# A DeepNorm layer with attention and retention heads: the norm of a retention head in two parts, key scaling and gating on ScalarE, gate rows turned by TensorE, first column sums read from the bank

## The chip, the core and the metric

The kernel runs on one core of a Trainium2 chip. A core has five engines that run side by side, each through its own list of instructions in order: TensorE (PE) multiplies matrices, VectorE (DVE), ScalarE (ACT) and GpSimd (POOL) work on tiles of 128 partitions, and SyncE (SP) issues transfers to 16 DMA engines. Results of PE land in PSUM, in banks of 128 x 512 float32, and a bank can be written again only when its readers are done. The metric is the device time of one execution in microseconds (us).

## The reference

One decoder layer over 1024 positions of width 1024, in float32. The part that the change touches is the conditioning and the retention heads:

```
mod = silu(c) @ w_ada + b_ada              # six rows of 1024: sh1, sc1, g1, sh2, sc2, g2
h = x * (1 + sc1) + sh1
proj = h @ w_in                            # 8 attention heads of 64 and 4 retention heads of 128
# retention, in chunks of 128 positions, per head:
q = q*cos + rotate_half(q)*sin;  k = (k*cos + rotate_half(k)*sin) * dk**-0.5
s = (q @ k.T) * inner                      # inner: decay of the head
o = s @ v + (q @ R) * xi
R = R * g_chunk + (k * zeta).T @ v
# then, per head and position:
o = (o - mean(o)) * rsqrt(var(o) + eps) * silu(g)
mix = concat(attention, o) @ w_out
x = layer_norm(alpha*x + g1*mix)           # then a gated MLP with a convolution, gated by g2, and a second norm
```

## The kernel before

A float32 product is made of three matmuls: each operand is split into a high and a low part in a format that PE multiplies at full rate, and high x high, high x low and low x high are added up in a bank. The low part of a weight or of h is a subtraction on DVE or POOL after a cast on ACT.

The program has one block (named r) that computes the conditioning, the four retention heads and the value projection of the attention heads; attention itself, the output projection and the MLP follow. Only block r is touched. Two things set the order in it. PE's instructions, most of DVE's and some of ACT's and SP's are chained in the order in which the code issues them (by `queued`, which shows as line 150 in the profile; `in_turn`, `turn` and `vec` call it). The others, among them ACT's copies out of the banks and POOL's products, are placed by a scheduler.

The block goes through these stages.

- **The condition row.** silu(c) stands in eight columns. DVE multiplies the identity by each column (tile `diag`), a matmul with ones spreads that as a row over all partitions (`csp`, a double bank), and ACT copies the two halves to `csb`. Before and after it PE multiplies a constant tile (`warm`) 6 and 11 times (`keep_on`).
- **The first head's first seven chunks** (`h_load`, `h_cast`, `h_sum`, `h_mod`, `h_lo`, `h_low`). For each j of 8 (128 features each), SP loads two pieces of w_ada (tiles `ada`, 512 KB each), 128 rows of the first head's weights (`wrr`) and of x transposed (`xt`). DVE sums ada times csb over the row into a column of scales and one of shifts (`h_sum`; it shows as ISA or CUSTOM_DVE). ACT scales xt into the high part `hhi`, DVE makes `hlo`, and PE adds 21 matmuls (7 chunks x 3) into seven banks (`fa`, `fb`). Near the end SP loads the second head's weights and small tables (`ret_consts`).
- **The retention loop**, m = 7 to 31, a chunk of a head in each. A chunk's projection is 24 matmuls (`rp`) in two half-steps, after each of which `emit(t)` issues what a table holds for half-step t. ACT copies the bank to a row tile `rst` (q, k, v, g, 128 columns each); POOL multiplies q and k by the sine (`rt`, lines 372 and 373), and DVE by the cosine and adds (`ret_spin`). `ret_a` turns q and k on PE (`pq`), copies them on ACT (`qkT`) and scales k by the decay on DVE (`kz`). `ret_b` multiplies k with q and kz with v (`pS`), and DVE makes `sT` (scores times decay) and the state `R`. `ret_c` makes the output `po`, from which DVE takes the mean and variance (`bs`, `mv`) and ACT a copy. `ret_swish` is a tanh on ACT and a product on DVE. At a head's end `ret_norm` makes the scale of its eight chunks (17 operations on 128x8 on DVE: `gt`, `gr`, `wg`), `ret_gate` normalises a chunk on DVE and multiplies it with its gate on POOL (line 464), and `ret_out` turns four chunks (`py`) and stores them. `mod_piece` sums one piece of the other four conditioning rows (`ada`) from step m = 10 on.
- **The value projection**, q = 0 to 15: 24 matmuls in a bank `vp`, from which ACT casts the high part and DVE subtracts the low part for four heads (`V`, lines 621 and 622). In the same steps come the last retention operations, the last column sums, and the load, cast and low part of the first attention head's weights (`wqkr`, `wqh`, `wql`).

The two rows g1 and g2 are needed as rows much later. They come out of the sums as columns (`gcol`, 128 x 8) and are stored by a transfer to `gates` that puts each element at its place.

The table of half-steps is made by these lines:

```
    A0, N0, O0, O1 = 3, 5, 3, 5
        ta = max(2 * n + A0, 2 * NT - 1 + (5 * n + 3) // 4)
        tb = ta + 1
        t_c = tb + (2 if late else 1)
```

where n counts a head's chunks through all heads, ta is the half-step of `ret_a`, tb of `ret_b`, t_c of `ret_c`. Within a half-step the operations are issued in the order of RANK.

## Time and profile before

| | |
|---|---|
| median of 3 runs | 1247.38 us (1246.58 to 1248.6) |
| the profiled execution | 1248.95 us, span 1247.2 us |
| mean granted clock of TensorE | 0.990 |
| PE busy | 1210.4 us, 97% of the span |
| DVE, ACT, POOL busy | 923.7, 631.4, 249.8 us |
| block r | from 0 to about 300 us: PE busy for 281.38 us of them |

The profile is of one execution. A line of a group or of the timeline names the kernel's line, the engine, the operation and the tiles (written tile, arrow, read tiles, without their numbers), then the shape and how many; brackets hold the idle time of the engine before it and what ended that. Lines 150 and 152 are those of the helper `queued`, so that groups there are told apart by tiles. PE is busy nearly all the time, and its clock, PEclk, is granted in parts of full speed: where PE waits, time goes, and after some waits the clock is lower for a while. The other engines' idle time is of no matter by itself.

### The profile page before, as it was taken

The numbers are of one execution on the slowest core, as the hardware profiler recorded it, in microseconds if no ns is written. First come the engines' busy times: TensorE is split into PE (matmuls) and PEld (weight loads), VectorE is DVE, ScalarE is ACT, GpSimd is POOL, SyncE is SP. The second block draws the span as 40 slices with busy tenths as digits, with TensorE's granted clock in tenths as the row PEclk, the third lists the DMA queues.
The fourth block names the chain that finished last, engine by engine and source line by source line (L and its number), as shares of the span: only waits on it lengthen the run. The fifth ranks groups of instructions, "written<-read, shape, count | busy, mean of one in ns | idle before, by whom it ended". The sixth has DMA issues, their size and how long they took to land.

```text
span 1247.2 us, 17036 instructions
## 1 busy us (share of the span) xinstructions
PE 1210.4 (97%) x5982; PEld 1008.4 (81%) x5982; DVE 923.7 (74%) x1784; ACT 631.4 (51%) x1131; POOL 249.8 (20%) x293
## 2 busy tenths in 40 slices
PE   7998999979999999999999999999999999999997
PEld 5887888978888887788788888888888878888885
DVE  7857758574877778746797877878778785886586
ACT  5533232233766668476764544544445554634452
POOL 0315143210333334300002221221100101000021
PEclk9999999989999999999899999999999999999999
DMA  9523344753234235323239877886544578965751
GB/s 355 214 75 120 110 153 136 146 101 111 85 95 151 77 102 180 107 94 109 85 111 227 188 175 202 202 192 179 133 130 132 150 249 247 348 224 192 264 185 68
DMA packets 88261, 199.77 MB, mean 160 GB/s; under 512 B 11952, under 2 KB 18288, under 8 KB 88176
## 3 DMA queue, kind: packets, MB, share of 16 engines
q1 hardware_dynamic: 75504, 175.62, 42.0%
q0 software_dynamic: 12672, 23.07, 11.7%
q8 instruction: 47, 0.77, 0.3%
q14 instruction: 38, 0.31, 0.1%
HBM read 165.06 MB, written 68.20 MB: 187 GB/s over the span
## 4 chain that ended last, share of the span: by engine, by line
PE 80%; DVE 10%; DMA 4%; ACT 3%; issue 2%; POOL 1%; DVEq 0%; SPq 0%; ACTq 0%; POOLq 0%
PE dX L1314 10%; PE rp L150 7%; PE dZ L1314 7%; PE uX L1130 6%; PE uX L1131 6%; PE uX L1132 6%; PE uY L1131 4%; PE uY L1132 4%; PE uY L1130 4%; PE pv L800 3%; PE qk L716 2%; PE qk L717 2%; PE qk L718 2%; PE pt L784 2%; DVE ada L150 2%
## 5 line engine op out<-in xcount | busy, mean ns | idle before, releaser
L150 PE MATMUL rp<-wr,hhi 128*128 128x512 f32 x400 | 129.1, 404 | 0.0
L1303 DVE TENSOR_TENSOR dl<-dr,dh 128x1024 fp32r<-128x1024 f32 x66 | 80.0, 1236 | 36.6 <-ACT dh L1291 36.3
L1291 ACT CAST dh<-dr 128x1024 fp32r<-128x1024 f32 x66 | 67.8, 1049 | 74.1 <-DMA dr<-in_w_down_dram 35.9
L762 POOL TENSOR_TENSOR S<-S,dn 128x128 f32<-128x128 f32 (+3 forms) x64 | 74.1, 1163 | 154.2 <-DVE dn L761 123.8
L977 POOL DMA_DIRECT2D sd<-gd x22 | 18.1, 824 | 397.3 <-DMA sd<-y 231.8
L150 PEld LDWEIGHTS rp<-wr,hhi 128*128 128x128 f32 x400 | 72.3, 190 | 13.0
L150 PE MATMUL rp<-wr,hlo 128*128 128x512 f32 x200 | 79.2, 396 | 0.0
L1314 PE MATMUL dX<-dl,dh 128*128 128x512 f32 x176 | 68.5, 389 | 0.0
L1314 PE MATMUL dX<-dh 128*128 128x512 f32 x176 | 68.5, 389 | 0.0
L1314 PE MATMUL dX<-dh,dl 128*128 128x512 f32 x176 | 68.5, 389 | 0.0
L150 DVE CUSTOM_DVE_ANT_0 ada<-ada,csb,bcol 128x1024 f32<-128x1024 f32 (+1 forms) x48 | 61.7, 1298 | 8.7 <-DMA ada<-in_ada_dram 5.1
L1145 ACT COPY u<-uX 128x512 f32<-128x512 f32 x44 | 25.8, 586 | 74.2 <-PE uX L1132 74.2
L758 ACT ACTIVATE S<-S,mn 128x128 f32<-128x128 f32 (+3 forms) x64 | 49.8, 779 | 15.6 <-DVE mn L753 14.3
L150 PE MATMUL vp<-wv,hhi 128*128 128x264 f32 (+1 forms) x256 | 50.8, 299 | 4.8 <-DVE gt L150 4.8
L716 PE MATMUL qk<-hhi,wqh 128*128 128x512 f32 x128 | 54.6, 427 | 0.0
L753 DVE CUSTOM_DVE_ANT_0 S<-ps,nb 128x128 f32<-128x128 f32 (+3 forms) x64 | 47.9, 750 | 8.4 <-PE ps L751 6.0
L791 DVE TENSOR_TENSOR pt<-pt,pt 128x512 fp32r<-128x512 f32 (+2 forms) x96 | 50.8, 550 | 4.3 <-ACT pt L790 3.1
L800 PE MATMUL pv<-pt,V 128*128 128x256 f32 x320 | 49.9, 293 | 2.4 <-DVE pt L791 1.2
L193 PE MATMUL op<-wol,mxs 128*128 128x512 f32 x128 | 50.4, 394 | 1.7 <-DVE wol L900 1.5
L718 PE MATMUL qk<-hhi,wql 128*128 128x512 f32 x128 | 51.7, 404 | 0.0
L192 PE MATMUL op<-woh,mxs 128*128 128x512 f32 x128 | 50.7, 398 | 0.9 <-DVE mn L753 0.9
L1314 PE MATMUL dZ<-dh 128*128 128x512 f32 x132 | 51.6, 391 | 0.0
(1040 smaller groups left out, 3670.2 us busy)
## 6 DMA issues: line engine op xcount, KB each, us to landing
ada<-in_ada_dram SPq DMA_DIRECT2D x48, 512.0 KB, 4.2
td<-in_w_down_dram SPq DMA_DIRECT2D x44, 256.0 KB, 5.8
wa<-in_w_up_dram SPq DMA_DIRECT2D x22, 512.0 KB, 5.5
wb<-in_w_up_dram SPq DMA_DIRECT2D x22, 512.0 KB, 4.9
gd<-y SPq DMA_DIRECT2D x22, 512.0 KB, 3.2
sd<-y SPq DMA_DIRECT2D x44, 256.0 KB, 3.6
dr<-sd SPq DMA_DIRECT2D x44, 256.0 KB, 3.9
dr<-td SPq DMA_DIRECT2D x44, 256.0 KB, 4.1
```

What stands on the lines that cost most here:

```text
L150: order[key] = fn(*args, **kw)
L716: nc.tensor.matmul(pt, whi[:, j, :], hhi[j][:, sl], start=(j == 0), stop=False)
L718: nc.tensor.matmul(pt, wlo[:, j, :], hhi[j][:, sl], start=False, stop=(j == ND - 1))
L762: nc.gpsimd.tensor_tensor(out=Ssb[:, :span], in0=Ssb[:, :span], in1=den.to_broadcast([P, span]), op=ALU.mult,)
L791: nc.vector.tensor_tensor(out=dl, in0=src, in1=f(dh), op=ALU.subtract)
L800: nc.tensor.matmul(pv[:, :256], V2[h][:, kb, :], pts[kb // 4][u][:, kb % 4, :], start=(kb == 0 and u == 0), stop=(kb == nkb - 1 and u == 1),)
L1130: nc.tensor.matmul(pt, whi, bh, start=start, stop=False, skip_group_check=True)
L1131: nc.tensor.matmul(pt, whi, bl, start=False, stop=False, skip_group_check=True)
L1132: nc.tensor.matmul(pt, wlo, bh, start=False, stop=stop, skip_group_check=True)
L1291: nc.scalar.copy(hi, raw)
L1303: nc.vector.tensor_tensor(out=lo, in0=raw, in1=f(hi), op=ALU.subtract)
L1314: nc.tensor.matmul(pt, w_[:, 0, q], m_[:, 1, :], start=start and n_ == 0, stop=stop and n_ == 2, skip_group_check=True)
```

## The change

The diff touches block r alone, in four places.

1. **Start.** The condition row lies in two tiles, a bank each, and the sums of the first piece read them from PSUM in halves, scale and shift in turn, without waiting for `csb` (`h_sum0`). The constant tile is set by POOL, `keep_on` is 5 and 9 matmuls, the two sums of the next piece go ahead of `h_lo`, and the loads of the second head's weights move forward (`w1_load`): two at j = 4 right behind x's last piece, two among the small tables.
2. **First head.** The sine products of its chunks 0 to 6 (14 operations) go from POOL to DVE, in `ret_spin`.
3. **Retention.** `kz` is made by ACT (28 operations). `ret_norm` is in two parts, one half-step apart: 7 operations, then 10, the last of which is new: mr = -mean x scale. With it a chunk is normalised by one ACT operation, scale x o + mr (32 operations, formerly on DVE). The output product comes two half-steps after the scores for each chunk, sT has three buffers, and in a half-step output, scores and turning come ahead of swish, gates and norm. Gates start two half-steps after the norm's first part, and the two output halves come at 4 and 6.
4. **Gate rows.** The columns of g1 and g2 are turned on PE (after q = 2 and q = 10), copied by ACT, and stored as 8 rows of 512 bytes (`mod_rows`).

DVE's list shows the third place around the first head's norm. In the names, gt, gr and wg are the norm's small tiles, mv the means and variances, mr the new tile, rst the row tiles, ISA with ada a column sum. Before, from the norm's tail to the next scores:

```order
L150 TENSOR_SCALAR wg_1014<-wg_1014 128x8
L150 TENSOR_TENSOR gr_1012<-gr_1012,wg_1014 128x8
L150 TENSOR_SCALAR gr_1012<-gr_1012,rc 128x8
L150 TENSOR_TENSOR rst_2_592<-rst_2_592,trig 128x256
L150 TENSOR_TENSOR rst_2_592<-rst_2_592,rt_5_991 128x2x64 x2
L150 ISA ada_0_3_938,mod_94<-ada_0_3_938,csb,bcol 128x1024
L150 ISA mod_94 128x1
L150 SCALAR_TENSOR_TENSOR rst_0_590<-rst_0_590 128x128
L150 TENSOR_SCALAR rst_0_497<-rst_0_497,mv_501,gr_1012 128x128 x2
L150 TENSOR_TENSOR sT_1_1064<-pS_1_1061,dec 128x128
L150 SCALAR_TENSOR_TENSOR R_1_1066<-R_0_976,rc,pS_1_1061 128x128
```

Here the norm of 17 operations stands in one piece, and a rotation, a column sum, a swish and two gates stand between it and sT. With the change, from a score to the next one:

```order
L152 TENSOR_TENSOR sT_1_1036<-pS_1_1033,dec 128x128
L152 SCALAR_TENSOR_TENSOR R_1_1038<-R_0_964,rc,pS_1_1033 128x128
L152 SCALAR_TENSOR_TENSOR rst_3_499<-rst_3_499 128x128
L152 TENSOR_SCALAR gt_1049<-mv_500,rc 128x8
L152 TENSOR_SCALAR gt_1049<-gt_1049,rc 128x8
L152 TENSOR_SCALAR gr_1050<-gt_1049 128x8
L152 TENSOR_TENSOR wg_1053<-gr_1050 128x8
L152 TENSOR_TENSOR wg_1053<-wg_1053,gt_1049 128x8
L152 TENSOR_SCALAR wg_1053<-wg_1053 128x8
L152 TENSOR_TENSOR gr_1050<-gr_1050,wg_1053 128x8
L152 TENSOR_TENSOR sT_2_1078<-pS_2_1075,dec 128x128
L152 SCALAR_TENSOR_TENSOR R_2_1080<-R_1_1038,rc,pS_2_1075 128x128
```

The norm's first part stands between two sT. Behind these rows come a swish, the second part (ten operations), a rotation and a column sum, then the next sT; no gate is in the list.

ACT's list at the same place of the program has the copies of a turned pair (qkT), the tanh (rst from rst alone), the casts of the third head's weights (wr) and the copies of outputs (rst from po). Before:

```order
L432 COPY rst_0_590<-po_1_1095 128x128
L392 COPY qkT_3_1112<-pq_3_1109 128x256
L439 ACTIVATE rst_1_591<-rst_1_591 128x128
L181 CAST wr_6_1124<-wrr_6_1122 128x512
L181 CAST wr_7_1127<-wrr_6_1122 128x512
L392 COPY qkT_4_1166<-pq_4_1163 128x256
L432 COPY rst_1_591<-po_2_1149 128x128
```

With the change, where L500 is the gate and kz the key scaling:

```order
L430 ACTIVATE kz_4_1148<-rst_2_591,rc 128x128
L426 COPY qkT_3_1085<-pq_3_1082 128x256
L471 ACTIVATE rst_1_590<-rst_1_590 128x128
L500 ACTIVATE rst_0_496<-rst_0_496,mr_1100,gr_1050 128x128 x2
L500 ACTIVATE rst_1_497<-rst_1_497,mr_1100,gr_1050 128x128 x2
L500 ACTIVATE rst_2_498<-rst_2_498,mr_1100,gr_1050 128x128 x2
L500 ACTIVATE rst_3_499<-rst_3_499,mr_1100,gr_1050 128x128 x2
L430 ACTIVATE kz_5_1226<-rst_2_591,rc 128x128
L426 COPY qkT_4_1146<-pq_4_1143 128x256
L471 ACTIVATE rst_2_591<-rst_2_591 128x128
L178 CAST wr_6_1110<-wrr_6_1108 128x512
```

The eight gates of the first head stand together, behind the turned pair of the second head's chunk 3 and ahead of the key scaling of chunk 5, the pair of chunk 4 and the casts of the weights.

SP's list shows the fourth place, in the value projection. Before, the store of the gates stands between column-sum loads and ahead of the load of the first attention head's weights:

```order
L542 DMA ada_3_1_2443<-in_ada_dram 128x1024
L542 DMA ada_3_2_2487<-in_ada_dram 128x1024
L169 DMA gates<-gcol 128x8x1
L542 DMA ada_3_3_2535<-in_ada_dram 128x1024
L542 DMA ada_3_4_2574<-in_ada_dram 128x1024
L591 DMA wqkr_2577<-in_w_qk_dram 128x1024
L542 DMA ada_3_5_2625<-in_ada_dram 128x1024
```

With the change:

```order
L577 DMA ada_3_1_2447<-in_ada_dram 128x1024
L577 DMA ada_3_2_2491<-in_ada_dram 128x1024
L577 DMA ada_3_3_2539<-in_ada_dram 128x1024
L577 DMA ada_3_4_2583<-in_ada_dram 128x1024
L634 DMA wqkr_2586<-in_w_qk_dram 128x1024
L585 DMA gates<-grow_2544 8x128
L577 DMA ada_3_5_2634<-in_ada_dram 128x1024
L577 DMA ada_3_6_2683<-in_ada_dram 128x1024
```

The store comes behind that weight load, and is one of 8 rows of 128 elements.

The diff, without the parts that only rename or move code:

```diff
@@ -217,8 +221,10 @@
         queued("SP", nc.sync.dma_start, tr, trig)
         rc = cp.tile([P, 3, RH], F32, tag="rc", name="rc")
         queued("SP", nc.sync.dma_start, rc, rcols)
+        w1_load(2)
         dec = slot("S", [P, RH, P], F32, "dec")
         queued("SP", nc.sync.dma_start, dec, decay)
+        w1_load(3)
         bfb = cp.tile([P, FH], F32, tag="bfb", name="bfb")
         queued("SP", nc.sync.dma_start, bfb, bcast_rows(b_f, FH))
         lnc = cp.tile([P, 2, ND], F32, tag="lnc", name="lnc")
@@ -249,10 +255,15 @@
...
-        cuts = h_cuts(j) if i == 0 else [slice(0, D)]
-        for sl in cuts:
-            queued("DVE", nc.vector.tensor_tensor_reduce, **row_sum(a, sl, out, first))
-            first = out
+        queued("DVE", nc.vector.tensor_tensor_reduce, **row_sum(a, slice(0, D), out, first))
+
+    def h_sum0(pcs):
+        for q in range(2):
+            for i in range(2):
+                out = mod1[:, 0, i:i + 1]
+                queued("DVE", nc.vector.tensor_tensor_reduce,
+                       **row_sum(hs[0][0][i], slice(512 * q, 512 * q + 512), out,
+                                 out if q else bcol[:, i, 0:1], pcs[q]))
...
@@ -285,59 +296,76 @@
...
-            in_turn(pc[:, co], ones, dg[:, sl, :].rearrange("p j q -> p (j q)"),
+            pcs.append(csp[q])
+            in_turn(pcs[q], ones, dg[:, sl, :].rearrange("p j q -> p (j q)"),
                     start=True, stop=True)
-            queued("ACT", nc.scalar.copy, csb[:, co], pc[:, co])
+            queued("ACT", nc.scalar.copy, csb[:, 512 * q:512 * q + 512], pcs[q])
+        return pcs
...
-    keep_on(6)
-    cond_rows()
...
-    keep_on(11)
+    keep_on(5)
+    pcs = cond_rows()
+    keep_on(9)
     h_cast(0)
-    h_sum(0, 0)
-    h_sum(0, 1)
+    h_sum0(pcs)
     h_low(0)
     h_mod(0)
...
+    def w1_load(q):
+        raw1[q] = slot("R", [P, 2, 512], F32, f"wrr1_{q}")
+        queued("SP", nc.sync.dma_start, raw1[q], w_ret[1, :, 2 * q:2 * q + 2, :])
...
     for j in range(ND):
         h_load(j + 3)
         if j + 1 < ND:
             h_cast(j + 1)
-            h_sum(j + 1, 0)
-        if j == 0:
-            h_lo(j)
-        if j + 1 < ND:
-            h_sum(j + 1, 1)
+            for i in range(2):
+                h_sum(j + 1, i)
         if j + 2 == ND:
-            ret_load(1, 0, w1)
+            w1_cast(0)
         if j + 1 < ND:
             h_mod(j + 1)
-        if j > 0:
-            h_lo(j)
+        h_lo(j)
         if j + 1 < ND:
             h_low(j + 1)
+        if j + 2 == ND:
+            w1_low(0)
+            w1_low(1)
+        if j + 4 == ND:
+            w1_load(0)
+            w1_load(1)
         if j + 3 == ND:
             tr, dec, rc, bfb, lnc, cw = ret_consts()
         if j + 1 == ND:
-            for q in range(2, ND, 2):
-                ret_load(1, q, w1)
+            for q in range(1, 4):
+                w1_cast(q)
             queued("SP", nc.sync.dma_start, cw, conv)
-            for w, raw in w1:
-                queued("DVE", nc.vector.tensor_tensor, out=w[:, 1, :], in0=raw,
-                       in1=f(w[:, 0, :]), op=ALU.subtract)
+            for k in range(2, ND):
+                w1_low(k)
             w1 = [w for w, _ in w1]
         hi, lo = hhi[j], hlo[j]
         for t in range(3):
@@ -369,12 +397,18 @@
...
-        nc.gpsimd.tensor_tensor(out=t2[:, :, 0, :], in0=qk[:, :, 1, :], in1=sb, op=ALU.mult)
-        nc.gpsimd.tensor_tensor(out=t2[:, :, 1, :], in0=qk[:, :, 0, :], in1=sb, op=ALU.mult)
-        st["spin", c] = (qk, cos, t2)
+        st["spin", c] = (qk, cos, t2, sb)
+        if (h, c) >= (0, NT - 1):
+            for b in range(2):
+                nc.gpsimd.tensor_tensor(out=t2[:, :, b, :], in0=qk[:, :, 1 - b, :], in1=sb,
+                                        op=ALU.mult)
 
     def ret_spin(c, st):
-        qk, cos, t2 = st.pop(("spin", c))
+        qk, cos, t2, sb = st.pop(("spin", c))
+        if st is sts[0] and c < NT - 1:
+            for b in range(2):
+                vec(nc.vector.tensor_tensor, out=t2[:, :, b, :], in0=qk[:, :, 1 - b, :],
+                    in1=sb, op=ALU.mult)
...
@@ -393,9 +427,7 @@
...
             kz = sp.tile([P, P], F32, tag="kz", bufs=2, name=f"kz{h}_{c}")
-            vec(nc.vector.tensor_scalar, out=kz, in0=row[:, P:2 * P], scalar1=rc[:, 0, h:h + 1], scalar2=None,
-                op0=ALU.mult,
-            )
+            nc.scalar.activation(kz, row[:, P:2 * P], AF.Copy, scale=rc[:, 0, h:h + 1])
             st["kz"] = kz
...
@@ -405,9 +437,9 @@
...
-        sT = sp.tile([P, P], F32, tag="sT", bufs=2, name=f"sT{h}_{c}")
+        sT = sp.tile([P, P], F32, tag="sT", bufs=3, name=f"sT{h}_{c}")
         vec(nc.vector.tensor_tensor, out=sT, in0=pS[:, 0:128], in1=dec[:, h, :], op=ALU.mult)
-        st["sT"] = sT
+        st["sT", c] = sT
...
@@ -440,27 +472,33 @@
...
-        r = small([P, NT], f"gr{h}")
-        rsqrt(r, t, NT, f"g{h}", lambda **kw: vec(nc.vector.tensor_scalar, **kw),
-              lambda **kw: vec(nc.vector.tensor_tensor, **kw))
...
-        st["r"] = r
+    def ret_norm(h, part, st):
+
+        if part == 0:
+            t, r = small([P, NT], f"gt{h}"), small([P, NT], f"gr{h}")
+            vec(nc.vector.tensor_scalar, out=t, in0=st["mv"][:, :, 1], scalar1=rc[:, 2, h:h + 1],
+                scalar2=None, op0=ALU.mult)
+            vec(nc.vector.tensor_scalar, out=t, in0=t, scalar1=rc[:, 2, h:h + 1], scalar2=GN_EPS,
+                op0=ALU.mult, op1=ALU.add)
+            st["root"] = [r, t, small([P, NT], f"wg{h}")]
+            root_seed(r, t, vec_scalar)
+            root_step(*st["root"], NT, vec_scalar, vec_tensor)
+            return
+        r, t, w = st["root"]
+        for _ in range(2):
+            root_step(r, t, w, NT, vec_scalar, vec_tensor)
+        vec(nc.vector.tensor_scalar, out=r, in0=r, scalar1=rc[:, 2, h:h + 1], scalar2=0.5,
+            op0=ALU.mult, op1=ALU.mult)
+        mr = small([P, NT], f"mr{h}")
+        vec(nc.vector.scalar_tensor_tensor, out=mr, in0=st["mv"][:, :, 0], scalar=-1.0, in1=r,
+            op0=ALU.mult, op1=ALU.mult)
+        st["r"], st["mr"] = r, mr
...
-        vec(nc.vector.tensor_scalar, out=o, in0=o, scalar1=st["mv"][:, c, 0:1], scalar2=st["r"][:, c:c + 1],
-            op0=ALU.subtract, op1=ALU.mult,
-        )
+        nc.scalar.activation(o, o, AF.Identity, scale=st["r"][:, c:c + 1],
+                             bias=st["mr"][:, c:c + 1])
...
@@ -501,7 +539,7 @@
...
-    A0, N0, O0, O1 = 3, 5, 3, 5
+    A0, N0, O0, O1 = 3, 5, 4, 6
...
@@ -511,9 +549,8 @@
...
-        late = ta == 2 * n + A0
         tb = ta + 1
-        t_c = tb + (2 if late else 1)
+        t_c = tb + 2
...
@@ -521,25 +558,31 @@
...
-        at(t, ret_norm, h, None)
+        for q in range(2):
+            at(t + q, ret_norm, h, q)
         for c in range(NT):
-            at(t + 1 + c // 2, ret_gate, h, c)
+            at(t + 2 + c // 2, ret_gate, h, c)
...
-    RANK = (ret_swish, ret_gate, ret_c, ret_b, ret_a, ret_norm, ret_out)
+    RANK = (ret_c, ret_b, ret_a, ret_swish, ret_gate, ret_norm, ret_out)
...
+    def mod_rows(m):
+
+        pt = bank(f"gT{m}")
+        turn(pt[:ND, :P], gcol[:, m, :], ident)
+        row = tmp([ND, P], F32, f"grow{m}")
+        nc.scalar.copy(row, pt[:ND, :P])
+        nc.sync.dma_start(gates[m:m + 1, :].rearrange("o (j p) -> (o j) p", p=P), row)
...
@@ -683,6 +726,8 @@
...
             mod_piece()
+        if q in (2, 10):
+            mod_rows(q // 8)
...
```

84 lines of the change are left out of this document (39 added, 45 removed).

## The prediction

> **What bounds the kernel now.** The profiled execution took 1248.95 us, with a span of 1247.2 us; the median of the three timed runs is 1247.38, so the profiled one stands 1.57 above it. I read the page's engine totals first (TensorE, PE, is busy for 97% of the span), then who PE waits for, then stretches of the block that the change touches, which ends near 300 us. The list of PE's waits gives the sum in us, the count and the longest:
>
> ```profile
> PE vp L150 <- DVE gt L150: 4.8, 1, 4.8
> ...
> PE po L150 <- DVE sT L150: 3.6, 1, 3.6
> ...
> PE py L150 <- POOL rst L464: 2.5, 3, 1.1
> PE fa L150 <- ACT hhi L150: 1.7, 2, 1.2
> ...
> PE pS L150 <- DVE kz L150: 1.4, 1, 1.4
> ...
> PE csp L150 <- ACT csb L152: 0.7, 1, 0.7
> ```
>
> These six sit in the block that is changed. The stretches show that PE has no idle time between them or after them, and what each long wait costs once more through the granted clock. Columns: stretch, length, busy time and count of PE, PEld, DVE, ACT, POOL, then PEclk, DMA share, GB/s:
>
> ```profile
> 62.90:108.00 45.10, 45.10 (x242) 38.82 (x243) 26.62 (x101) 15.24 (x41) 10.81 (x17) 1.00 0.29 94
> 120.00:254.00 134.00, 134.00 (x774) 116.89 (x772) 85.82 (x276) 39.45 (x115) 43.73 (x68) 1.00 0.52 144
> 276.00:300.00 24.00, 24.00 (x177) 22.84 (x177) 10.34 (x61) 7.12 (x32) 0.00 (x0) 1.00 0.28 60
> ...
> 114.00:116.00 2.00, 2.00 (x6) 1.52 (x6) 1.97 (x6) 1.41 (x4) 0.36 (x2) 0.50 0.09 37
> 116.00:118.00 2.00, 2.00 (x10) 1.60 (x9) 2.00 (x4) 0.11 (x1) 2.00 (x2) 0.74 0.00 0
> ...
> 259.00:261.00 2.00, 1.99 (x9) 2.00 (x10) 1.86 (x15) 0.76 (x4) 0.00 (x0) 0.50 0.76 225
> 261.00:263.00 2.00, 2.00 (x11) 2.00 (x11) 0.68 (x6) 1.13 (x3) 0.00 (x0) 0.50 0.09 37
> ...
> 267.00:269.00 2.00, 0.79 (x4) 0.28 (x2) 2.00 (x5) 0.21 (x1) 1.84 (x3) 1.00 0.00 0
> ...
> 271.00:273.00 2.00, 2.00 (x12) 2.00 (x11) 2.00 (x11) 1.50 (x8) 1.46 (x4) 0.50 1.34 73
> ```
>
> So a microsecond taken from a wait in this block should reach the end of the block, and the clock loss goes with the wait. Lost time is length times one minus PEclk. After the 3.6 us wait: 2 x 0.50 + 2 x 0.26 = 1.5, and about 0.2 at its edges, 1.7. After the 4.8 us wait: 2 x 0.50 twice, and some 0.4 in the next two microseconds, 2.4. After the three waits at 267 to 271: 1.0 and about 0.7, 1.7. The 1.4 us wait is followed by a clock of 1.00.
>
> The Trainium skill (TensorE: Matmul & The Clock Gate, HAM oscillation) puts the limit for keeping the clock at idle gaps of about 3.4 us. The first two waits agree with that. The third place does not: no gap there is over 1.1 us and the clock still fell to 0.50; the measurement decides, so I charge it.
>
> **The change part by part.**
>
> *Start (A).* The first column sums wait for the copy of the condition row, and the second half of that row waits for the first copy, because both share one double bank:
>
> ```profile
> 8.88 0.75 DVE L150 CUSTOM_DVE_ANT_0 ada<-ada,csb,bcol 128x512 f32<-128x512 f32 x1 [3.58 <-ACT csb L152]
> ...
> 13.55 1.19 PE L150 MATMUL fa<-wr,hhi 128*128 128x512 f32 x4 [1.15 <-ACT hhi L150]
> ...
> 44.76 1.14 ACT L150 CAST wr<-wrr 128x512 fp32r<-128x512 f32 x2 [3.31 <-DMA wrr<-in_w_ret_dram]
> 45.80 1.24 ACT L150 ACTIVATE hhi<-xt,mod 128x1024 fp32r<-128x1024 f32 x1
> ...
> 47.96 1.07 PE L150 MATMUL fa<-wr,hhi 128*128 128x512 f32 x4
> ...
> 8.00:47.00 39.00, 36.59 (x157) 28.15 (x157) 32.47 (x49) 25.42 (x28) 0.00 (x0) 1.00 1.03 402
> ```
>
> Reading the bank takes out a copy (0.6) and the wait for it (0.7), and the four half sums interleaved take another 1.2 to 2 out of the front, so the first matmul may start up to 3 us sooner. That is not what the stage gains, because it ends on data: the DMA share is 1.03 from 8 to 47 us. The last piece's scaled rows (hhi at 45.80, done 47.05) stand behind a cast on ScalarE that waited 3.31 us for the second head's weights; PE begins with that piece at about 47.75. The weights now go ahead of the trigonometric table; one load of 512 KB at 402 GB/s is 1.3 us. So hhi can be done at about 45.75, and PE gains at most 0.7 + 1.3 = 2.0. Bounds: 0 (the load lands where it did) to 2.0. I take 1.7, nearer the upper end, since the landing follows from the queue's order alone.
>
> *Rotations of the first head (B).* Fourteen sine products go from POOL to DVE, and the key scaling goes to ScalarE:
>
> ```profile
> 60.49 0.90 DVE L150 TENSOR_TENSOR rst<-rst,rt 128x128 f32<-128x128 f32 x2
> ...
> 62.57 0.27 DVE L150 TENSOR_SCALAR kz<-rst,rc 128x128 f32<-128x128 f32 x1
> ...
> 63.21 0.49 DVE L150 TENSOR_TENSOR rst<-rst,rt 128x128 f32<-128x128 f32 x2
> ...
> 59.78 0.68 DVE L150 TENSOR_TENSOR rst<-rst,trig 128x256 f32<-128x256 f32 x1
> 61.32 0.41 DVE L150 TENSOR_TENSOR rst<-rst,trig 128x256 f32<-128x256 f32 x1
> ```
>
> While POOL multiplies, a chunk costs DVE 0.68 + 0.90, about 1.55 with overlap; alone it costs 0.41 + 0.49. Two more products of the same size add about 0.6 (the pair of 0.49, plus overheads), so a chunk takes 1.5 either way: no loss, and no wait for POOL's first product. The key scaling stands at 62.57 behind five chunks of rotations; on ScalarE, busy for 15.24 of the next 45.10 us, it can follow its own chunk. PE's 1.4 us wait goes, unless ScalarE's copies of rows are ahead: 0 to 1.4, and -1 if DVE does fall behind. I take 1.2.
>
> *First head's norm (C).* PE's 3.6 us wait (3.55 unrounded, to 112.2) is for sT, the decayed scores. What DVE did meanwhile:
>
> ```profile
> 103.00 0.44 DVE L150 TENSOR_SCALAR gt<-mv,rc 128x8 f32<-128x8 f32 x1
> ...
> 106.54 0.23 DVE L150 TENSOR_SCALAR gr<-gr,rc 128x8 f32<-128x8 f32 x1
> ...
> 107.55 2.33 DVE L150 CUSTOM_DVE_ANT_0 ada<-ada,csb,bcol 128x1024 f32<-128x1024 f32 x1
> ...
> 109.81 1.33 DVE L150 SCALAR_TENSOR_TENSOR rst<-rst 128x128 f32<-128x128 f32 x1
> 111.07 0.88 DVE L150 TENSOR_SCALAR rst<-rst,mv,gr 128x128 f32<-128x128 f32 x2
> 111.88 0.28 DVE L150 TENSOR_TENSOR sT<-pS,dec 128x128 f32<-128x128 f32 x1
> ...
> 541.38 2.91 ACT L848 ACTIVATE hr<-nT,AB 128x128 f32<-128x128 f32 x8 [2.05 <-PE nT L845]
> ```
>
> Seventeen small operations (103.00 to 106.77), rotations, a column sum, the swish and two gates stood ahead of sT. Now sT comes first in each step, seven small operations stand before the next sT and ten after it (one is new, 0.2 us), and no gate is on DVE. The most that DVE has between two sT is then 7 x 0.21, or 10 x 0.21 with a rotation and a sum, 2 + 0.9 + 2.3 = 5.3 us against 9 before; with the output product a half-step later for every chunk, PE does not come to it first. The whole 3.55 + 1.7 = 5.25 should go. Its price is on ScalarE: eight gates follow each other there, and eight operations of that form and size (scale and bias from columns) took 2.91 us in the row above. Behind them stand the fifth key scaling, the fourth transposed pair and the casts of weights 6 and 7. The gates can start when the norm ends, about 112.0, so the pair would come at about 115.3 to 115.7, and PE wants it at about 115.75, by the matmuls that stand between in its order, at the pace of the stretch from 62.9 to 108. I charge 0.9 (0 to 1.7): gain 4.35, between 0 and 5.25.
>
> The Trainium skill (ScalarE: Activation LUTs, What ACT_TABLE_LOAD costs) prices column operands on this engine at some 93 ns each, which speaks against the move: from its figures a gate is 0.48 us and eight in a row an estimated 3.2. By that the charge at C would be 1.2 and the sum 0.3 less; the row decides.
>
> *Gates turned (D).* PE's longest wait, 4.8 at 259.0, is labelled with a norm operation, but the bank that vp needs is freed by a subtraction on DVE that is late. Its chain begins at a store:
>
> ```profile
> 236.50 0.38 SPq L169 DMA_DIRECT2D gates<-gcol  x1
> ...
> 240.16 0.33 SPq L591 DMA_DIRECT2D wqkr<-in_w_qk_dram  x1
> ...
> 242.00:244.00 2.00, 2.00 (x19) 2.00 (x19) 2.00 (x8) 0.78 (x4) 0.00 (x0) 1.00 0.72 31
> 244.00:246.00 2.00, 2.00 (x19) 2.00 (x18) 0.33 (x3) 0.00 (x0) 0.00 (x0) 1.00 1.06 39
> ...
> 253.04 1.05 ACT L594 CAST wqh<-wqkr 128x1024 fp32r<-128x1024 f32 x1 [10.13 <-DMA wqkr<-in_w_qk_dram]
> ...
> DMA to landing us min/median/max: 3.5/5.0/12.8
> ```
>
> The store writes 1024 pieces of 4 bytes. After it the DMA engines are full at 31 to 39 GB/s, and the weight load issued at 240.16 lands after 12.8 us, where its like takes 5.0. ScalarE stands 10.13 us in that cast, the copies of V behind it are late, and with them PE. As a row store there are eight pieces of 512 bytes, issued behind the weight load. The load then lands at about 245, the cast is done at 246, and V of the group before is out before PE asks at 254.3. Added: two transposes (0.2 each on PE), two copies (0.3 each on ScalarE). Gain 4.75 + 2.4 = 7.15, less 0.15, 7.0; bounds 0 (something else holds the load) to 7.15.
>
> *Last gates (E).* PE's turning of the fourth head waits for POOL's products:
>
> ```profile
> 268.63 1.88 POOL L464 TENSOR_TENSOR rst<-rst 128x128 f32<-128x128 f32 x2 [0.16 <-DVE rst L150]
> ```
>
> Each takes 0.94 here, beside a column sum on DVE. The gates come from ScalarE now, and sooner, as D has gone. Four products at up to 0.95 behind a norm that ends 1 to 2 us ahead of the transposes leave 1.6 to 3 us of the wait. Cost before 2.5 + 1.7 = 4.15 with rounding; I leave 2.15 and take 2.0 (0 to 4.15).
>
> Together 1.7 + 1.2 + 4.35 + 7.0 + 2.0 = 16.25. The changed kernel's profiled execution would take 1248.95 - 16.25 = 1232.7, and its median, 1.57 lower, **1231** us.
>
> **The rivals.**
>
> *All stalls go.* If A and E give their upper ends and C is not charged: 2.0 + 1.4 + 5.25 + 7.15 + 4.15 = 19.95, so 1227.4 us. For it: the gaps are single waits with nothing behind them. Against: POOL's products stay on POOL.
>
> *The load stays late.* If the weight load was slow for another reason than the 4-byte pieces, such as the three sum rows of 512 KB around it, D gives nothing: 16.25 - 7.0 = 9.25, 1238 us. Against it: the engines are full at 31 GB/s, which loads of large rows, 402 GB/s at the start, do not show.
>
> *Slower: the run of gates on ScalarE.* ScalarE works in order. If the eight gates hold its queue until the norm's last operation and 2.9 us more at each head, the transposed pair comes after PE's slot and PE pays a wait like today's (3.55 + 1.7 = 5.25) at each of four heads. Today only head 0 pays: three more are 15.75 lost, and C and E give nothing. With A, B and D at 9.9 that is 5.85 slower, 1253 us. It decides from a hold of more than a half-step, 3.4 us. For it: head 0 is at its margin. Against: heads 1 and 2 have fewer retention steps per matmul, and ScalarE is busy for 39.45 of 134 us there.
>
> *Given back later.* If attention after 300 us is set by something that this block does not move, what PE gains it waits for there: about 1247. Against it: 24.00 of 24.00 us busy in the stretch to 300, and 97% over the span.
>
> **How the numbers follow.** Forecast 0.60; all stalls go 0.14; the load stays late 0.14; slower 0.06; given back 0.06. The range 1226 to 1241 holds the first three, 0.88, with the spread of C and E, and leaves the rest out. About 0.2% (2.5 us) is what a measurement of this kernel can tell from no change. Faster: 0.60 + 0.14 + 0.14 and a little of the last, 0.89; within: 0.05; slower: 0.06.
>
> **What would show it.** Right: PE's list no longer has the waits of po for sT and vp for gt; PEclk is 1.00 from 112 to 120 and 255 to 265; the weight load lands in about 5 us; a wait of py for POOL of 1 to 3 us remains. A: stage one's last matmul ends 1.5 to 2 us sooner, not 3. Wrong: a wait of pS or po for qkT on ScalarE near 115 us of over 2 us, a wait of vp again, or new waits in the attention stage that add up to the gain.

## The result, and the profile after

The changed kernel took 1231.35 us (median of 4 runs, 1230.62 to 1232.44) where the kernel before took 1247.99 us (4 runs beside it): the ratio is 0.9868, with a 95% interval of 0.9851 to 0.9885. In a later group on another chip it took 1230.74 us against 1249.03: 0.9851 (0.9833 to 0.9868). The forecast was 1231. The profiled execution took 1230.62 us with a span of 1228.9 us.

PE's waits in the changed kernel, the longest of the whole execution, in the columns of the list before (sum in us, count, longest):

```profile
PE fb L154 <- POOL warm L290: 2.8, 1, 2.8
PE uY L1175 <- ACT ht L874: 2.6, 1, 2.6
PE fa L152 <- ACT hhi L152: 2.1, 2, 1.5
...
PE vp L152 <- POOL wv L525: 1.0, 1, 1.0
...
PE pS L152 <- ACT qkT L426: 0.8, 1, 0.8
...
PE vp L152 <- ACT wv L524: 0.3, 1, 0.3
```

The first line is PE's wait for its constant tile at the start (4.1 before), the second lies far behind the block (2.6 before too), the third is in stage one (1.7 before). The waits of po for sT, of pS for kz, of vp for V (labelled gt) and of py for POOL's gates are gone. Three new ones stand in block r: 0.8 for a turned pair, and 1.0 and 0.3 for the last weights of the value projection. Two positions of PE tell what the block gained, the first projection matmul after stage one and the transpose that ends the block. Before:

```profile
52.72 0.61 PE L150 MATMUL rp<-wr,hhi 128*128 128x512 f32 x2
...
293.25 0.27 PE L150 MATMUL pcumT<-ident,cum 128*64 128x128 f32 x1
```

After:

```profile
50.99 0.62 PE L152 MATMUL rp<-wr,hhi 128*128 128x512 f32 x2
...
275.71 0.27 PE L152 MATMUL pcumT<-ident,cum 128*64 128x128 f32 x1
```

Stage one ends 1.73 us sooner and the block 17.54 us sooner. The rest of the kernel keeps that: the two profiled spans differ by 18.3 us. What lies behind the block varies by more than this difference of 0.8: a second profiled execution of the changed kernel, below, ends the block at 275.13 and has a span of 1232.7 us. In the attention stage PE waits there 1.9 us for one tile (`mixF`), and 0.9 in the first profile, a wait that the kernel before does not show. So in what follows a change of one or two microseconds is read from the end of the block, where two profiles of one kernel differ by 0.6, and the times carry the larger ones.

The stretches where the clock had been at half speed, and the two places of the new waits (columns as before; PE's busy time is the second number, PEclk the third from the end):

```profile
112.00:114.00 2.00, 1.17 (x8) 0.90 (x7) 1.52 (x8) 2.00 (x8) 2.00 (x5) 1.00 0.24 20
114.00:116.00 2.00, 2.00 (x11) 1.71 (x12) 1.41 (x3) 2.00 (x7) 2.00 (x4) 1.00 0.60 246
...
226.00:228.00 2.00, 0.92 (x6) 0.51 (x4) 0.00 (x0) 1.59 (x4) 1.11 (x1) 1.00 0.48 164
...
256.00:258.00 2.00, 2.00 (x20) 2.00 (x19) 1.97 (x12) 1.35 (x9) 2.00 (x6) 1.00 0.00 0
258.00:260.00 2.00, 2.00 (x20) 2.00 (x19) 1.88 (x14) 0.99 (x6) 0.35 (x1) 1.00 0.40 131
```

PEclk is 1.00 in all of them: the new waits cost their length and no clock. The timeline shows the price at the first head's norm (ACT's gates, what follows them, PE's wait):

```profile
110.06 3.19 ACT L500 ACTIVATE rst<-rst,mr,gr 128x128 f32<-128x128 f32 x8 [3.36 <-DVE mr L152]
113.15 0.39 ACT L430 ACTIVATE kz<-rst,rc 128x128 f32<-128x128 f32 x1
113.44 0.35 ACT L426 COPY qkT<-pq 128x256 f32<-128x256 f32 x1
...
113.84 0.49 PE L152 MATMUL pS<-qkT 128*128 128x128 f32 x2 [0.83 <-ACT qkT L426]
```

Eight gates take 3.19 us, the pair's copy ends at 113.79, and PE starts at 113.84. The weight load and the last gates, by the queue, ACT, POOL and PE:

```profile
234.90 0.33 SPq L634 DMA_DIRECT2D wqkr<-in_w_qk_dram  x1
...
239.35 1.05 ACT L637 CAST wqh<-wqkr 128x1024 fp32r<-128x1024 f32 x1 [1.94 <-DMA wqkr<-in_w_qk_dram]
...
253.49 4.86 POOL L502 TENSOR_TENSOR rst<-rst 128x128 f32<-128x128 f32 x8 [24.48 <-ACT rst L500]
...
257.05 0.60 PE L152 MATMUL py<-ident,rst 128*128 128x128 f32 x4
```

The load is cast 4.45 us after its issue, against 12.88 before. POOL's eight products take 0.61 us each and begin 3.6 us ahead of PE's turning.

### The profile page after: what moved, and what is told of

The parts are those of the page before. It is cut to its first block, busy times and chain, and to the rows that moved or that the text cites. A ratio compares the mean times of both kernels' runs of the same rounds, so it can differ in the third digit from the quotient of the medians.

```text
span 1228.9 us, 17048 instructions
## 1 busy us (share of the span) xinstructions
PE 1202.9 (98%) x5981; PEld 1002.7 (82%) x5981; DVE 906.2 (74%) x1743; ACT 651.4 (53%) x1193; POOL 241.9 (20%) x280
## 4 chain that ended last, share of the span: by engine, by line
PE 77%; DVE 8%; DMA 7%; ACT 3%; issue 2%; POOL 2%; SPq 0%; DVEq 0%; POOLq 0%; ACTq 0%
PE dX L1359 10%; PE dZ L1359 7%; PE uX L1176 6%; PE uX L1175 6%; PE uX L1177 6%; PE uY L1177 4%; PE uY L1176 4%; PE uY L1175 4%; PE rp L152 4%; PE vp L152 4%; DMA ada<-in_ada_dram 3%; PE pv L845 3%; PE qk L761 2%; PE qk L762 2%; PE qk L763 2%
## 5 line engine op out<-in xcount | busy, mean ns | idle before, releaser
L152 DVE CUSTOM_DVE_ANT_0 ada<-ada,csb,bcol 128x1024 f32<-128x1024 f32 x46 | 59.5, 1298 | 3.4 <-DMA ada<-in_ada_dram 3.4
L1359 PE MATMUL dZ<-dl,dh 128*128 128x512 f32 x132 | 51.4, 389 | 0.0
```

The source lines that it names most:

```text
L152: order[key] = fn(*args, **kw)
L1359: nc.tensor.matmul(pt, w_[:, 0, q], m_[:, 1, :], start=start and n_ == 0, stop=stop and n_ == 2, skip_group_check=True)
```

## The experiments

All runs in one table. "Ratio" is to the kernel before, timed on the same chip in the same group; "stage one" and "block" are the starts of the two PE instructions above in the run's own profile.

| run | median us | before us | ratio (95%) | stage one | block |
|---|---|---|---|---|---|
| before | 1247.38 | | | 52.72 | 293.25 |
| changed | 1231.35 | 1247.99 | 0.9868 (0.9851 to 0.9885) | 50.99 | 275.71 |
| column store | 1240.24 | 1251.02 | 0.9911 (0.9891 to 0.9930) | 50.97 | 285.82 |
| before, row store | 1241.26 | 1251.02 | 0.9927 (0.9905 to 0.9948) | 52.97 | 286.34 |
| norm whole, gates on DVE | 1233.39 | 1251.02 | 0.9856 (0.9833 to 0.9879) | 50.58 | 277.94 |
| gates spread | 1229.69 | 1251.02 | 0.9827 (0.9805 to 0.9848) | 50.45 | 273.43 |
| changed, again | 1230.74 | 1249.03 | 0.9851 (0.9833 to 0.9868) | 50.67 | 275.13 |
| output early | 1233.35 | 1249.03 | 0.9871 (0.9855 to 0.9887) | 50.87 | 276.83 |
| later output only | 1232.53 | 1249.03 | 0.9864 (0.9849 to 0.9880) | 50.53 | 276.45 |
| loads late | 1232.19 | 1249.03 | 0.9863 (0.9846 to 0.9881) | 53.66 | 278.35 |
| spread, early weights | 1227.80 | 1251.52 | 0.9808 (0.9792 to 0.9823) | 50.28 | 272.02 |
| gates on DVE | 1231.63 | 1251.52 | 0.9838 (0.9822 to 0.9854) | 50.39 | 274.89 |
| key scaling on DVE | 1230.41 | 1251.52 | 0.9831 (0.9815 to 0.9847) | 50.66 | 275.36 |
| sums from the copy | 1230.47 | 1251.52 | 0.9833 (0.9817 to 0.9849) | 50.76 | 274.39 |

### The column store put back

```diff
-        if q in (2, 10):
-            mod_rows(q // 8)
...
     def mod_part(m, j, a):
...
+        if m > 1 and j == ND - 1:
+            nc.sync.dma_start(gates[m - 2:m - 1, :].rearrange("o (j p) -> p (o j)", p=P),
+                              gcol[:, m - 2, :])
```

> The changed kernel with the gate rows stored again as columns, in pieces of 4 bytes, with no turning; all else as changed. If the small pieces are what held the weight load, its landing goes from 7.5 us at most back to over 11 us, PE waits 4 to 5 us for V's bank and loses 2 us of clock: 1237.5 to 1239. If the last gates' stall was a consequence of that delay, it returns with it: about 1242. If the column-sum loads around it held the weight load, 1231 as changed.

The time was 1240.24 us and the block ended at 285.82, 10.1 later than in the changed kernel's first profile and 10.7 later than in its second. The queue, the DMA rate behind the store, the landing times of the eight weight loads and PE's wait:

```profile
230.75 0.39 SPq L172 DMA_DIRECT2D gates<-gcol  x1
...
234.43 0.33 SPq L637 DMA_DIRECT2D wqkr<-in_w_qk_dram  x1
...
236.00:238.00 2.00, 2.00 (x19) 2.00 (x18) 1.94 (x8) 0.78 (x5) 0.00 (x0) 1.00 0.97 43
238.00:240.00 2.00, 2.00 (x19) 2.00 (x18) 0.58 (x3) 0.00 (x0) 0.00 (x0) 1.00 1.07 45
240.00:242.00 2.00, 2.00 (x19) 2.00 (x18) 0.00 (x0) 0.00 (x0) 0.00 (x0) 1.00 0.92 35
...
DMA to landing us min/median/max: 3.4/5.0/15.2
...
255.68 0.78 PE L152 MATMUL vp<-wv,hhi 128*128 128x264 f32 x2 [7.79 <-DVE gt L152]
```

With the same loads of column sums around it, the column store alone brings back full engines at 35 to 45 GB/s, a load that lands after 15.2 us, and a wait of 7.79. It also stands ahead of the weight load again, and no run stores rows at that place; that the pieces count and not the place rests on the rate, since behind the changed kernel's row store (issued at 237.28) the engines are busy for 0.14 of 238 to 240 us. The wait is longer than the 4.8 of before, since PE now comes 6.4 us sooner (247.89 for 254.26) to a load that lands only 3.3 sooner (249.6 for 253.0). PE does not wait for the last gates in this run: the late load alone does not bring their wait back.

### The row store alone, in the kernel before

```diff
-        if m > 1 and j == ND - 1:
-            nc.sync.dma_start(gates[m - 2:m - 1, :].rearrange("o (j p) -> p (o j)", p=P),
-                              gcol[:, m - 2, :])
...
+        if q in (2, 10):
+            mod_rows(q // 8)
```

> The kernel before with the gate rows turned and stored as rows, and nothing else of the change. If the small pieces alone hold the load, 7 us less than before, about 1241. If the last gates' wait and its clock loss (4.2 us) hang on that delay too, 11 us less, about 1237. If the split norm and ScalarE's gates are needed for the last gates, the wait of py for POOL stays at 2 to 3 us. If the loads around hold it, 1248 as before.

The time was 1241.26, and the block ended at 286.34, 6.9 sooner than before (7.2 sooner counted from the end of stage one, which was 0.25 later). The wait for V's bank is gone, and the last gates still cost PE three waits and the clock behind them:

```profile
PE py L150 <- POOL rst L461: 1.8, 3, 1.1
...
259.58 1.89 POOL L461 TENSOR_TENSOR rst<-rst 128x128 f32<-128x128 f32 x2 [24.60 <-DVE rst L150]
...
260.80 0.27 PE L150 MATMUL py<-ident,rst 128*128 128x128 f32 x1
...
265.00:267.00 2.00, 2.00 (x11) 2.00 (x11) 1.84 (x11) 0.73 (x5) 0.62 (x2) 0.50 0.21 66
```

So D and E are two things. Counted from the last output product ahead of the wait for V (247.82 before, 248.75 here) to the first turning of the last gates (267.13 and 260.80), the row store saves 7.26 us. Here POOL begins 1.2 us ahead of PE and takes 0.94 for a product; in the changed kernel it begins 3.6 us ahead and takes 0.61.

### The norm whole and the gates on DVE

```diff
-            root_step(*st["root"], NT, vec_scalar, vec_tensor)
-            return
-        r, t, w = st["root"]
-        for _ in range(2):
-            root_step(r, t, w, NT, vec_scalar, vec_tensor)
+            for _ in range(3):
+                root_step(*st["root"], NT, vec_scalar, vec_tensor)
+        else:
+            return
...
-        nc.scalar.activation(o, o, AF.Identity, scale=st["r"][:, c:c + 1],
-                             bias=st["mr"][:, c:c + 1])
+        vec(nc.vector.tensor_scalar, out=o, in0=o, scalar1=st["mv"][:, c, 0:1], scalar2=st["r"][:, c:c + 1],
+            op0=ALU.subtract, op1=ALU.mult,
+        )
```

> The changed kernel with the norm's operations in one piece again, in the half-step of its first part, and the gates normalised on DVE; order within a half-step, later outputs and three sT buffers stay. If the pile on DVE is what made PE wait for sT, the 3.6 us wait and 1.7 us of clock return at head 0, less the 0.8 us wait for ScalarE: 4.4 more, about 1235.7. If the later output product and the new order within the half-step suffice, 0 to 1 more.

No wait for sT came back at the first head, nor the 0.83 for ScalarE. The theory that the shorter pile on DVE is what removed the wait did not hold in this form. What the run lost is mostly at the third head's turning, where POOL's products came late (0.28 and 1.37; by the list of waits 1.9 in three) and the clock fell behind them, which cost 1.7 us more. The block ended 2.2 to 2.8 us later than in the changed kernel's two profiles. The time, 1233.39, is in the same direction, but its interval overlaps that of the changed kernel.

### The gates spread

```diff
-        nc.scalar.copy(qkT, pq[:, 0:256])
+        queued("ACT", nc.scalar.copy, qkT, pq[:, 0:256])
...
-        nc.scalar.activation(o, o, AF.Identity, scale=st["r"][:, c:c + 1],
-                             bias=st["mr"][:, c:c + 1])
+        queued("ACT", nc.scalar.activation, o, o, AF.Identity, scale=st["r"][:, c:c + 1],
+               bias=st["mr"][:, c:c + 1])
```

> The changed kernel with ScalarE's gates and its copies of the turned pairs chained in the order of the code, so that gates stand in pairs behind a half-step's copies instead of eight in a run. If the run of gates is what made PE wait 0.83 us at 113.8 us, that wait goes and the time is 0.8 less, about 1230.5. If it costs as much elsewhere (copies held behind gates that wait for the norm), 1231 to 1233.

The wait for the turned pair is gone, the one for the last value weights fell from 1.0 to 0.5, and the block ended at 273.43, 1.7 to 2.3 sooner. The time was 1229.69. So the 0.83 us was the price of eight gates in a run.

### The changed kernel again, and the output product early

The first of the next group is the changed kernel without an edit.

> The changed kernel itself, so that the others of this group have it on their chip: within 1 us of 1231 if the chips agree, and in the profile the same waits (0.8 us for ScalarE's turned pair, 1.3 us for the last value weights).

It took 1230.74 us and showed the same waits in the block. The second takes back only the extra half-step between the scores and the output.

```diff
-        t_c = tb + 2
+        t_c = tb + (2 if ta == 2 * n + A0 else 1)
```

> The changed kernel with the output product at its half-step of before (one after the scores in the first two heads), everything else as changed: norm in two parts, gates on ScalarE. If the shorter pile on DVE is what removed PE's wait for sT at the first head's norm, the wait stays under 1.2 us and the time is 0 to 1 us above the changed kernel's. If the extra half-step removed it, a wait of 2 to 3.5 us is back, with clock loss 3 to 5 us more.

PE waited for sT twice: 0.83 us at 63.46, behind the first scores, and 0.29 at the first head's norm; the block ended 1.1 to 1.7 later than the changed kernel's. Here the split, the gates on ScalarE and the new order within the half-step carry C without the later output; which of the three does it is not shown.

### The later output alone

```diff
-    RANK = (ret_c, ret_b, ret_a, ret_swish, ret_gate, ret_norm, ret_out)
+    RANK = (ret_swish, ret_gate, ret_c, ret_b, ret_a, ret_norm, ret_out)
```

and the norm whole with gates on DVE, as in the run above.

> The changed kernel with the norm in one piece, gates on DVE, and swish and gates ahead of output and scores in a half-step as before; of the retention part only the later output product, the three sT buffers and the key scaling on ScalarE stay. If the extra half-step alone removes PE's wait for sT, no such wait, and PE waits for POOL's last products 1 to 2 us: 2 to 3.5 us above the changed kernel. If the order within the half-step is needed too, a wait for sT of over 1 us at the first head's norm: 4 us or more above.

No wait for sT here either. Two rows of DVE at the first head's norm show why:

```profile
102.80 0.22 DVE L152 TENSOR_SCALAR gt<-mv,rc 128x8 f32<-128x8 f32 x1
...
108.98 0.28 DVE L152 TENSOR_TENSOR sT<-pS,dec 128x128 f32<-128x128 f32 x1
```

sT is still 6.2 us behind the norm's first operation (8.9 before: 103.00 to 111.88), but PE wants it a half-step later. The 2.7 us came off because the norm's place in the table hangs on the last output: it moved by a half-step too, and a rotation and a column sum now stand ahead of it and not between it and sT. The block ended at 276.45, 0.7 to 1.3 later than the changed kernel's, with 1.3 us of short waits for POOL's products. C was cured twice: the half-step does it with the norm whole and the gates on DVE, and the split, the gates on ScalarE and the order do it without the half-step. No run takes back both in the changed kernel; the two kernels that have neither, before and with the row store alone, wait 3.55 and 3.65 us, but they lack the other edits as well.

### The second head's loads late

```diff
-        if j + 4 == ND:
-            w1_load(0)
-            w1_load(1)
...
-        w1_load(2)
+        w1_load(0)
+        w1_load(1)
         dec = slot("S", [P, RH, P], F32, "dec")
         queued("SP", nc.sync.dma_start, dec, decay)
-        w1_load(3)
+        w1_load(2)
+        w1_load(3)
```

> The changed kernel with the loads of the second head's weights behind the small tables, as before, and the new start. If the last piece of stage one is set by that load through the cast on ScalarE, PE's 0.58 us wait before the last piece grows by one load (1.3 us at 400 GB/s) to 1.6 to 1.9, and the time by 1.0 to 1.3. If the front alone gives the gain, no change.

The wait came as the theory has it, 1.92 us behind the cast that waits for the load, but stage one ended at 53.66: 2.7 to 3.0 later than in the changed kernel, and 0.9 later than before the change. The rows show the rest:

```profile
44.82 1.14 ACT L152 CAST wr<-wrr 128x512 fp32r<-128x512 f32 x2 [3.30 <-DMA wrr<-in_w_ret_dram]
...
47.16 1.99 PE L152 MATMUL fa<-wr,hhi 128*128 128x512 f32 x4 [1.92 <-ACT hhi L152]
...
46.00:48.00 2.00, 0.84 (x2) 0.75 (x3) 0.77 (x2) 1.97 (x2) 0.00 (x0) 0.82 0.74 260
48.00:50.00 2.00, 2.00 (x6) 1.52 (x5) 1.59 (x2) 2.00 (x5) 0.00 (x0) 0.50 0.05 17
50.00:52.00 2.00, 2.00 (x8) 1.59 (x8) 2.00 (x5) 1.49 (x3) 0.00 (x0) 0.83 0.00 0
```

The clock fell to 0.50 behind a gap of 1.92 us: some 0.36 + 1.0 + 0.34 = 1.7 us lost, which I had not priced. The time was 1232.19 beside 1230.74; the intervals overlap, and the block ends 2.6 to 3.2 later.

### Sums from the copy

```diff
-    h_sum0(pcs)
+    h_sum(0, 0)
+    h_sum(0, 1)
...
-        queued("DVE", nc.vector.tensor_tensor_reduce, **row_sum(a, slice(0, D), out, first))
+        cuts = h_cuts(j) if i == 0 else [slice(0, D)]
+        for sl in cuts:
+            queued("DVE", nc.vector.tensor_tensor_reduce, **row_sum(a, sl, out, first))
+            first = out
```

> The changed kernel with the first column sums reading the copied row again, one after the other, the loads as changed. The first matmul comes 1 to 2.5 us later. If stage one ends on data alone, the 0.58 us wait before its last piece takes up the delay and the stage ends at most 0.6 later. If PE's own chain of 8 x 21 matmuls binds as well, the stage ends 0.5 to 1.9 later, the delay less those 0.58 us.

The first matmul came at 12.01 instead of 11.09, and stage one ended at 50.76, between the changed kernel's 50.99 and 50.67. The changed kernel's wait of 0.58 us before the last piece is not there: it took up most of the delay. The delay is hardly clear of chance: in the runs that leave the start as changed, the first matmul comes at 10.51 to 11.88, and with the loads as changed the stage ends at 50.28 to 50.99 without following it. Reading the sums from the bank shows no gain here; with the run before it, the stage ends on data.

### Key scaling on DVE

```diff
-            nc.scalar.activation(kz, row[:, P:2 * P], AF.Copy, scale=rc[:, 0, h:h + 1])
+            vec(nc.vector.tensor_scalar, out=kz, in0=row[:, P:2 * P], scalar1=rc[:, 0, h:h + 1], scalar2=None,
+                op0=ALU.mult,
+            )
```

> The changed kernel with the key scaling on DVE again. If its place behind the rotations on DVE made the second matmul of the first scores wait, a wait of pS for kz of about 1.4 us is back near 60 us and the block ends 1.2 to 1.5 later: about 1232. If the sine products' move to DVE (no wait for POOL's first product) was what removed it, no wait and the same time.

By the list, PE waited 0.7 us for kz, but not where the 1.4 us wait of before stood (62.90). The rows of this run, the first scores and then the first head's norm:

```profile
51.74 0.49 DVE L152 TENSOR_TENSOR rt<-rst,trig 128x128 f32<-128x128 f32 x2
...
59.23 0.28 DVE L152 TENSOR_SCALAR kz<-rst,rc 128x128 f32<-128x128 f32 x1
...
59.57 0.49 PE L152 MATMUL pS<-rst,kz 128*128 128x128 f32 x2
...
113.31 0.44 DVE L152 TENSOR_SCALAR kz<-rst,rc 128x128 f32<-128x128 f32 x1
...
113.80 0.49 PE L152 MATMUL pS<-qkT 128*128 128x128 f32 x2 [0.71 <-DVE kz L152]
```

At the first scores the scaling ends at 59.51 and its matmul starts at 59.57: B's wait stays away with the scaling on DVE. The 0.71 takes the place of the 0.83 for the turned pair, whose copy ends at 113.74 here, within 0.01 us of the scaling. The block ended at 275.36, as the changed kernel's. So the move of the key scaling did not remove B's wait. In both kernels it stands behind five chunks, which take 7.40 us before (55.17 to 62.57) and 7.49 here; what changed is when DVE begins them. The row of the kernel before:

```profile
55.17 0.67 DVE L150 TENSOR_TENSOR rst<-rst,trig 128x256 f32<-128x256 f32 x1 [0.78 <-POOL rt L373]
```

Counted from the end of stage one, that is 2.45 us before and 1.08 here. Of the 1.37 us between them, 0.78 is DVE's wait for POOL's products, which went with the sine products, and the other 0.6 is the low parts of the second head's weights, of which DVE now does two ahead of stage one's last piece. No run takes either back alone. The wait itself is not of one size: with the row store alone, the same code up to there, it is 0.68.

### Gates on DVE

The gate's two lines as in the run with the norm whole; the split stays.

> The changed kernel with the gates normalised on DVE again, everything else (norm in two parts, later output, row store) as changed. If the gates' place on DVE, behind column sums and low parts of V, made POOL's last products late, PE's waits for POOL come back: 1 to 2 us and their clock loss, 1.5 to 3.5 above the changed kernel. If the norm's split freed the last gates, no such wait and less than 1 us difference. At head 0 no wait for sT in either case.

At the last head PE does not wait, though DVE makes the gates: POOL's first product starts 2.9 us ahead of the turning. At the third head it waits 0.36 and 1.37:

```profile
209.21 0.49 POOL L503 TENSOR_TENSOR rst<-rst 128x128 f32<-128x128 f32 x1 [0.17 <-PE pq L152]
209.66 1.32 POOL L526 TENSOR_TENSOR wv<-wvr,wv 128x520 fp32r<-128x520 f32 x1
210.95 0.45 POOL L503 TENSOR_TENSOR rst<-rst 128x128 f32<-128x128 f32 x1
...
211.46 0.33 PE L152 MATMUL py<-ident,rst 128*128 128x128 f32 x1 [1.37 <-POOL rst L503]
```

A low part of the value weights stands between two products on POOL. In sum that is made up by the waits that the run does not have (0.83 for the pair, 1.3 for the value weights): the block ended at 274.89 and the time was 1231.63. So the last head's wait was not cured by the gates' move. The gaps at the third head are nearly those of the run with the norm whole, but here the clock stayed at 1.00 behind them.

### Spread gates and earlier value weights

```diff
-        if h > 0 and 3 <= c < 7:
-            if h < RH - 1:
-                ret_load(h + 1, 2 * (c - 3), nws)
-            else:
-                v_load(2 * (c - 3))
+        if 0 < h < RH - 1 and 3 <= c < 7:
+            ret_load(h + 1, 2 * (c - 3), nws)
+        if h == RH - 1 and 2 <= c < 6:
+            v_load(2 * (c - 2))
```

on top of the spread gates.

> The changed kernel with ScalarE's gates and turned pairs chained in the order of the code (as in the run with spread gates), and the value weights' loads one chunk earlier in the last head. If PE's two new waits (0.83 for the turned pair, 0.98 + 0.33 for the last value weights) are all that the change cost, both go: 2.1 us less in the block, about 1229 where the changed kernel takes 1231. If the earlier loads push column sums or rotations back through the shared buffers, a wait returns elsewhere and it stays at 1230 to 1232.

All three new waits are gone, PE was busy throughout 224 to 228 us, and the block ended at 272.02, 3.1 to 3.7 sooner than the changed kernel's. The time was 1227.80, a ratio of 0.9808 (0.9792 to 0.9823) to the kernel before, whose interval lies clear of both of the changed kernel's. It beats both kernels.

## Why the prediction was right, and where it was not

**What bounds the kernel.** PE's waits in one block, each with its clock, were the right place to count: the block ended 17.54 us sooner against a sum of 16.25, and the work behind it kept that. The rival that attention gives it back is refuted. That the median came within 0.4 us of the forecast is in part luck: the profiled execution, for which the sum was made, was to take 1232.7 and took 1230.62, and below a surplus and an omission cancel in part.

**A, the start: 1.7 forecast, 1.73 measured.** The reason holds too; in the second profile it is 2.05. The front came 2.46 us sooner (11.09 against 13.55), and the run with the sums from the copy shows no worth in its last 0.9 us. The rest of it and the loads' order are needed together: with the loads late PE waits 1.92 us for the last piece, and before the change it came to that piece without a wait (47.96, the data done at 47.05), so that sooner loads alone would have moved nothing. That last is argued from the rows; no run has the loads without the front. What the order insures was under-priced: without it the wait costs its clock as well, 2.7 to 3.0 us.

**B, the rotations: 1.2 forecast, the 1.4 us wait gone.** The size is right and the cause, in the main, is not. The step put the wait to the key scaling's place on DVE, behind five chunks; with the scaling put back there the wait stays away. DVE begins those chunks 1.37 us sooner after stage one: 0.78 because it does not wait for POOL's first product, which the step names beside it, and 0.6 because of low parts done sooner, which it does not count.

**C, the first head's norm: 4.35 forecast, about 4.4 measured** (the 3.55 us wait and 1.7 of clock, less a new wait of 0.83, where I had charged 0.9). The size is right and the reason incomplete. I put it to DVE's shorter pile and mentioned the half-step beside it; by the runs either is enough without the other, with the rest of the change in place. The clock's part is not fixed: behind the same wait the kernel with the row store alone was at half speed for 5.7 us of PE's work, a loss of 2.9. The row I used for eight gates gave 2.91 us, and they took 3.19. The figures of the Trainium skill (ScalarE: Activation LUTs, What ACT_TABLE_LOAD costs) had given an estimate of 3.2, and here that estimate was nearer than the row.

**D, the gates turned: 7.0 forecast, 7.2 measured** with the row store alone in the kernel before, and 10 with the column store alone put back into the changed one. The rival that other loads held the weights is refuted by both. The difference of 3 is what such a wait costs when PE comes to it 6.4 us sooner and the load only 3.3.

**E, the last gates: 2.0 forecast, about 4.2 measured.** That is the term that was mis-sized: 17.54, less 1.73, 1.4, 4.4 and 7.2, plus the 1.3 us of new waits for the value weights, leaves 4.1. By positions it is 4.0: from the last output product ahead of V's wait to the end of the block, the kernel with the row store alone takes 37.59 us (248.75 to 286.34) and the changed one 33.59 (242.12 to 275.71). I left 2.15 us of the wait, with POOL's products at 0.95 behind a norm that ends 1 to 2 us ahead. The products took 0.61, and the norm's last operation ended at 252.86, 4.2 us ahead of the turning at 257.05. What gave that lead is, by the runs, the table's half-step: the turning comes one half-step after its old place while the norm starts where it did. With the row store alone the norm ends 2.9 us ahead (2.2 before) and PE waits 1.8 us; with gates on DVE but the new table, PE does not wait there, and with the norm whole too it waits 0.6 at most. No run takes back the half-step alone. I had not counted that half-step, 24 matmuls and about 2.9 us, in E.

**What was missed.** The prediction does not say what is late next, and something was: the last weights of the value projection. PE came to the value projection 7.7 us sooner (223.74 for 231.48), and their last load, issued at 221.89 for 228.32 and cast at 226.19, only 6.4 sooner: 1.3 us of wait. E's surplus covers this; that the two cancel in part is luck.

**The slower rival.** ScalarE's run of eight gates held PE at one head, for 0.83 us and without clock loss. The condition that I gave, a hold of more than a half-step (3.4 us), did not decide it: ScalarE stood 3.36 us for the norm and then 3.19 in the gates, 6.6 in all, and PE lost 0.83. PE had turned the pair only by 109.81, so that 3.1 us of the hold were past before the pair could be copied, and the pair then stood for 3.6.

## What to carry to other kernels

Before a stall is costed, see which of the edits removes it alone: here two edits removed the same wait, and the gates' move to another engine, which looked like the core of one of them, was worth nothing in the sum. When an edit is taken back and a wait of the old name returns, look where it stands: that for kz came back 50 us behind its old place. Store a column of single elements as rows, by a transpose on TensorE, when anything else is to be loaded at that time. After an early stall is gone, walk along the engine that gains for the next thing that does not move up as far as it does, such as a load in a ring of buffers: the 1.3 and 0.83 us found so gave 3 us when mended.
